# A decoder layer in fp32 on one core: both tiles of an MLP step in one two-bank accumulator, operands and closing norms in larger batches

## The chip, the cores and the metric

The kernel runs on one core of a Trainium2 chip. The metric is the time of one execution on the device in microseconds (us). Before the change three runs took 2319.26, 2319.26 and 2327.7 us, so the median is 2319.26 us.

## What is computed

One step of a hybrid decoder layer on 2048 prompt tokens and 8 single-token samples, all in fp32, width 1024. The first half of the layer mixes tokens (four mLSTM heads of 128 and a causal pooling mixer between an input and an output projection). The second half is the MLP with a hidden width of 4096, which takes most of the time and all of the change:

```python
mix = jnp.einsum('blm,md->bld', mix, w_out)
x = x + ga1 * _rmsnorm(mix, g_post1)

hn2 = _rmsnorm(x, g_pre2) * (1.0 + sc2) + sh2
f = jnp.square(jax.nn.relu(jnp.einsum('bld,df->blf', hn2, w_up)))
f = jnp.einsum('blf,fd->bld', f, w_down)
x = x + ga2 * _rmsnorm(f, g_post2)
```

## The kernel before, in words

**Two phases.** The tokens go in four blocks of 512. Phase one computes the token mixer of all blocks and stores the result x1 in DRAM (`x1_d`). Phase two runs the MLP on block 0 (with the 8 samples joined to it, so its tiles are 260 columns wide where those of the others are 256), then on blocks 1, 2 and 3.

**Seven products.** Each MLP matrix product is done in the block form that needs seven products instead of eight, named P1 to P7. The right operands of the seven are b11, b21, b22 and four sums and differences of quarters of the normed input (`operand_steps`, line 495); the left ones are pieces of the weights, four of which were combined in phase one. `CHAIN` gives each product an accumulator: a takes P1, P6, P7, P4, b takes P2, c takes P5, P3. A product adds to its accumulator and the running sum is read between two products, so the next product on chain a has to wait until the sum before it was read.

**Three matmuls for one.** Every fp32 factor is split into a high and a low half (`split`, line 116: ACT copies the high half, DVE subtracts to get the low one), and every matmul is done as high x high, high x low, low x high. So each weight piece `raw` of 128x1024 gets one ACT copy (`whi`) and one DVE subtraction (`wlo`), with three buffers each.

**The MLP's order.** `mlp_steps` (line 223) writes the order of a block by hand: four chunks of 14 up steps (two groups g0, g1 of seven products) and 14 down steps. A step is 24 matmuls of 256 or 260 columns, or, in the down steps of blocks 1 to 3, 12 of 512. An up step works on two tiles of the hidden width, the pairs, one after the other: `up_step` (line 1351) gives each pair a PSUM bank of its own (`mm` and `ml`, three each), and `up_use` (line 1371) does the vector work of each pair by itself on tiles of 128x256: copies u1, u2, u3 out of chain a, relu squared into `quads`, the sums of the down operands into `sums`, and the halves into `f`. Down products P5, P6, P7 and P3 need the halves of `sums`, which are made only after the up products P4 and P3 of the group. `down_t_step` and `down_step` (lines 1427, 1449) add each result to the tiles `acc`.

**Steps in between.** Generators in the list `steps` are advanced by `tick()` between matmuls. The operands of the next block come that way in four rounds of one pair of k-tiles, begun in the last chunk (line 1531). Block 0's first four operands are made in the last block of phase one (line 1269); for the other three `operand_steps` runs a second time after phase one (lines 1331 to 1333), which loads and norms x1 and transposes its 32 tiles again. The scheduler may move instructions of an engine where the data allow it.

**Closing.** For blocks 1 to 3 `last_adds` (line 1509) squares each finished half tile on ACT, multiplies it on POOL, and `finish_norm` (line 560) takes a reciprocal square root for each 128-token tile by some ten DVE instructions on 128x1 and adds the residual. Block 0's result is transposed, so `finish_t` (line 1476) transposes it back, in one stretch after the block.

Of the kernel before, what the change touches and what calls it, by code (L numbers as in the profile page):

```python
# [17 lines left out]
P = 128  # L18
# [43 lines left out]
def layer_kernel(  # L62
# [30 lines left out]
    ps = ctx.enter_context(tc.tile_pool(name="ps", bufs=3, space=PSUM))  # L93

    def bank(tag, bufs):
        return ps.tile([P, 512], F32, name=tag, tag=tag, bufs=bufs)

    def mm_bank():
        return bank("mm", 3)

    def tr_bank():
        return bank("tr", 2)

    def ml_bank():
        return bank("ml", 3)
# [247 lines left out]
    selb = const.tile([NR, P], F32, name="selb")  # L353
    pool.tensor_copy(out=selb, in_=sel[:, 0:1].broadcast_to([NR, P]))

    warm = const.tile([P, 1], F32, name="warm")
    act.activation(out=warm, in_=one_t, func=AF.Tanh)
    scT = const.tile([P, KT, QP], F32, name="scT")
# [5 lines left out]
    bgate = const.tile([P, 2 * H], F32, name="bgate")  # L364
    gate_w = [const.tile([P, KT, 2 * H], F32R, name=f"gate_w{i}") for i in range(2)]
# [11 lines left out]
    def mod_load(u):  # L377
        raw = fetched.pop(0)
        rt = small.tile([NR, UC], F32, name="rt", bufs=2)
# [78 lines left out]
    def prenorm_steps(part, tiles, sample, xh, xl):  # L458
# [14 lines left out]
        for half in range(2):  # L473
# [4 lines left out]
            for k2 in range(KT // 2):  # L478
# [5 lines left out]
                for kk in range(2):  # L484
                    k = 2 * k2 + kk
                    yt = rows.tile([P, TS // 2], F32, name="yt", bufs=2)[:, :2 * P]
# [8 lines left out]
    def operand_steps(b, ops, products, room):  # L495
# [4 lines left out]
        if sample:  # L500
            xt = scale_rows(load_rows(x1_d[S:], NS), NS)
        xts = [scale_rows(load_rows(src, P), P) for src in x1_tiles(b)]
        for j in products:
            n = X_ORDER.index(j)
            t = (acts.tile([P, H, BUF + TS], F32R, name="uext", bufs=1) if n == PRODUCTS - 1 else
                 acts.tile([P, 4, TS], F32R, name=("hi4", "lo4")[n % 2])).rearrange("p a b -> p (a b)")
            ops[j] = t[:, :8 * SH].rearrange("p (c k t) -> p c k t", c=2, k=4)
        yield
        if sample:
            tp = tr_bank()  # L510
            for k in range(KT):
                pe.transpose(tp[:, k * NS:(k + 1) * NS], xt[:NS, k * P:(k + 1) * P], ident[:NS, :NS])
# [4 lines left out]
        for kt in range(4):  # L517
            top, low, ta, tb = room()
            for k, y in ((kt, top), (kt + 4, low)):
                tp = tr_bank()  # L520
                for i, xt in enumerate(xts):
                    pe.transpose(tp[:, i * P:(i + 1) * P], xt[:, k * P:(k + 1) * P], ident)
                act.activation(out=y[:, :, :HT], in_=tp.rearrange("p (h t) -> p h t", h=2), func=AF.Identity,
                               scale=sc_c[:, 1, k, 0:1], bias=sh_c[:, 1, k, 0:1])
                if sample:
                    pool.tensor_copy(out=y[:, :, HT:], in_=ys[:, k].rearrange("p (h n) -> p h n", h=2))
            yield
            b11, b12, b21, b22 = (y[:, h, :w] for y in (top, low) for h in range(2))
            t1, t2, t3, t4 = (t[:, h, :w] for t in (ta, tb) for h in range(2))
# [3 lines left out]
            if P7 in products:  # L533
                dve.tensor_tensor(out=t3, in0=b22, in1=b12, op=ALU.subtract)
            if P4 in products:
                dve.tensor_tensor(out=t4, in0=b21, in1=t2, op=ALU.subtract)
            for n, j in enumerate(products):
                split(ops[j][:, 0, kt, :w], ops[j][:, 1, kt, :w], src[j])
                if n % 3 == 2:
                    yield  # L540
            yield

# [211 lines left out]
    with tc.tile_pool(name="p1c", bufs=1) as p1c, tc.tile_pool(name="p1", bufs=1) as p1:  # L754
# [99 lines left out]
        def phase_one_room():  # L854
            y = [p1.tile([P, BUF + T], F32, name=n) for n in ("ps_a", "ps_b")]
            y += [p1.tile([P, TS], F32, name="pd", bufs=2) for _ in range(2)]
            return [t[:, :2 * SH].rearrange("p (h t) -> p h t", h=2) for t in y]
# [41 lines left out]
        def sample_heads(q, k, hvs):  # L899
# [53 lines left out]
            num = p1.tile([P, H, HD + 1], F32, name="num", bufs=2)[:NS]  # L953
# [11 lines left out]
            def ready(b):  # L965
# [3 lines left out]
                km = p1.tile([P, H, HD + 1], F32, name="w", bufs=2)[:NS, :, :HD]  # L969
# [33 lines left out]
        for b in range(NB):  # L1003
# [71 lines left out]
            def chunk_weights(c):  # L1075
# [11 lines left out]
                w = p1.tile([P, H, HD + 1], F32, name="w", bufs=2)[:, :, :P]  # L1087
# [26 lines left out]
            def chunk_heads(c, w, ae):  # L1114
                t0, t1 = c * P, (c + 1) * P
                num = p1.tile([P, H, HD + 1], F32, name="num", bufs=2)
# [150 lines left out]
            else:  # L1267
                xops = {}
# [307 lines left out]
```

## Time and profile before

| What | Value |
|---|---|
| median of three runs | 2319.26 us |
| the profiled execution, its own time | 2322.08 us |
| its span in the profile | 2320.4 us |
| mean granted clock of TensorE | 0.972 of full speed |
| phase one's last matmul; PE goes on with block 0 | 890.2 us; 931.6 us |
| block 1, block 2, block 3 begin | 1289, about 1645, about 1985 us |
| last matmul | 2305.6 us |

The profiled execution is 2.8 us longer than the median. [...] Almost all instructions are issued by one helper, so nearly every row names line 54 and the tiles tell which step it is: `raw`, `whi`, `wlo` are weights, `f` the halves of the hidden tiles, `u`, `quads`, `sums` the vector work between, `hi`, `lo`, `uext` the operands, `acc` the sums of the output, `xt` rows of x1, `tr` transposes.

### The profile page before, as it was taken

To read this page: it belongs to the slowest core of one execution; us is meant where nothing else is said; L and a number is where in the kernel's file an instruction comes from. 1 tells how busy PE (TensorE), PEld (TensorE's weight loads), DVE (VectorE), ACT (ScalarE), POOL (GpSimd) and SP (SyncE) were. 2 spreads that over 40 slices of the span, in tenths; PEclk is the share of its full clock that TensorE was granted. 3 is DMA by queue.
4 is the path that set the end of the run, shared out by engine and by line. 5 is a ranking of instruction groups with operands and counts; after the bars stand their busy time and mean duration, and the time that the engine had idled before them with its cause. 6 is when DMAs were issued, how large, how long until landed. Compare 5 with 4: busy or idle time off the path is not lost. (4 is left out here: it accounts for less than half of the span.)

```text
span 2320.4 us, 37926 instructions
## 1 busy us (share of the span) xinstructions
PE 2194.2 (95%) x14106; PEld 1923.7 (83%) x14106; DVE 1757.3 (76%) x3750; ACT 1166.9 (50%) x2047; POOL 114.9 (5%) x169
## 2 busy tenths in 40 slices
PE   7999999999999996899998899998999998999997
PEld 6997788787887775899998888987888987888995
DVE  4356867866784787867778988779978779968878
ACT  4342534533442355654546555546655547555554
POOL 2000000000000000000000300000100000100002
PEclk9997999999999997999999999999999999999998
DMA  8741487489479855465454655655755555655563
GB/s 278 223 144 54 136 294 258 157 274 309 150 223 298 269 167 192 138 193 159 153 188 148 226 185 168 195 184 172 235 192 181 183 184 171 215 190 180 176 224 123
DMA packets 270524, 451.78 MB, mean 195 GB/s; under 512 B 17377, under 2 KB 171146, under 8 KB 270330
## 3 DMA queue, kind: packets, MB, share of 16 engines
q1 hardware_dynamic: 270339, 449.36, 59.8%
q8 instruction: 111, 1.82, 0.3%
q14 instruction: 74, 0.61, 0.1%
HBM read 394.31 MB, written 55.21 MB: 194 GB/s over the span
## 5 line engine op out<-in xcount | busy, mean ns | idle before, releaser
L54 DVE TENSOR_TENSOR wlo<-raw,whi 128x1024 fp32r<-128x1024 f32 (+1 forms) x562 | 691.3, 1236 | 266.2 <-ACT whi L54 255.0
L54 ACT CAST whi<-raw 128x1024 fp32r<-128x1024 f32 (+1 forms) x562 | 585.4, 1047 | 599.0 <-PE ml L54 399.3
L54 PE MATMUL mm<-hi,whi 128*128 128x256 f32 (+2 forms) x1408 | 378.1, 322 | 14.0 <-ACT whi L54 7.8
L54 PE MATMUL mm<-lo,whi 128*128 128x256 f32 (+2 forms) x1408 | 370.8, 316 | 1.5 <-DVE rs_t L54 1.5
L54 PE MATMUL mm<-hi,wlo 128*128 128x260 f32 (+2 forms) x1024 | 336.5, 329 | 6.2 <-DVE wlo L54 6.0
L54 PEld LDWEIGHTS mm<-hi,whi 128*128 128x128 f32 x1408 | 242.4, 191 | 36.6 <-ACT whi L54 10.2
L54 PE MATMUL mm<-whi,f 128*128 128x512 f32 x672 | 246.1, 403 | 14.1 <-ACT whi L54 13.7
L54 PEld LDWEIGHTS mm<-lo,whi 128*128 128x128 f32 x1408 | 242.4, 191 | 19.6 <-ACT whi L54 1.6
L54 PE MATMUL ml<-whi,f 128*128 128x512 f32 x672 | 243.9, 398 | 0.0
L54 PEld LDWEIGHTS mm<-hi,wlo 128*128 128x128 f32 x1024 | 195.4, 191 | 28.3 <-DVE wlo L54 9.9
L54 PEld LDWEIGHTS mm<-whi,f 128*128 128x128 f32 x672 | 126.6, 190 | 56.4 <-ACT whi L54 21.6
L54 PEld LDWEIGHTS ml<-whi,f 128*128 128x128 f32 x672 | 127.2, 189 | 29.7
L54 PE MATMUL ml<-hi,whi 128*128 128x256 f32 (+1 forms) x768 | 142.5, 283 | 3.2 <-ACT u L54 3.2
L54 PE MATMUL mm<-wlo,f 128*128 128x512 f32 x336 | 134.6, 401 | 10.6 <-DVE wlo L54 10.6
L54 PE MATMUL ml<-lo,whi 128*128 128x256 f32 (+1 forms) x768 | 141.9, 282 | 0.0
L54 PE MATMUL ml<-wlo,f 128*128 128x512 f32 x336 | 133.6, 398 | 0.0
L54 PEld LDWEIGHTS ml<-hi,whi 128*128 128x128 f32 x768 | 118.6, 189 | 4.1 <-ACT u L54 4.0
L54 PEld LDWEIGHTS ml<-lo,whi 128*128 128x128 f32 x768 | 118.5, 189 | 0.0
L54 PE MATMUL mm<-lo,wlo 128*128 128x256 f32 (+1 forms) x384 | 109.5, 285 | 1.4 <-DVE wlo L54 1.3
L54 PE MATMUL mm<-f,whi 128*128 128x260 f32 x448 | 96.4, 304 | 13.9 <-ACT f L54 10.9
L54 PE MATMUL ml<-lo,wlo 128*128 128x256 f32 (+1 forms) x384 | 108.6, 283 | 0.0
L54 PE MATMUL ml<-hi,wlo 128*128 128x256 f32 (+1 forms) x384 | 108.6, 283 | 0.0
(383 smaller groups left out, 4439.0 us busy)
## 6 DMA issues: line engine op xcount, KB each, us to landing
raw<-in_w_up_dram SPq DMA_DIRECT2D x128, 512.0 KB
raw<-up_s SPq DMA_DIRECT2D x128, 512.0 KB
raw<-in_w_down_dram SPq DMA_DIRECT2D x104, 512.0 KB
raw<-dn_s SPq DMA_DIRECT2D x96, 512.0 KB
raw<-in_w_in_dram SPq DMA_DIRECT2D x80, 512.0 KB
raw<-in_w_ada_dram SPq DMA_DIRECT2D x32, 512.0 KB
xt<-x_d SPq DMA_DIRECT2D x32, 512.0 KB
raw<-dn_s SPq DMA_DIRECT2D x64, 256.0 KB
```

The lines of the kernel that those rows point to most:

```text
L54: ins = op(*args, **kwargs)
```

## The change

PSUM is dealt anew in phase two: three tiles of two banks, chain0 to chain2, each holding both pairs, instead of six single banks. `turn()` rotates which of them serves as a, b and c. A step's vector work is done once for both pairs, on 128x2x256, after the second pair's matmuls; the tiles u1 to u3 and `quads` give way to `qa` and `qb`. The order of the steps changes, and the halves are written product by product. The operands of blocks 1 to 3 come in two rounds of two k-tiles, with one square-root chain for four tiles (`scale_block`). Block 0's operands are all made inside phase one: five get their halves there, and those of P4 and P3 are kept as fp32 (`held`) and split at its end. Closing norms take two tiles at once, and `finish_t` becomes a step generator that runs beside block 1's up steps.

```diff
-            out += up(g0, P1, P2, P6, P5, P7) + up(g1, P1) + up(g0, P4, P3) + up(g1, P2, P6, P5, P7)
-            if b == 0:
-                out += down((P1, 0)) + up(g1, P4, P3)
-                out += down(*[(j, 0) for j in (P5, P6, P2, P7, P3, P4)])
-                out += down(*[(j, 1) for j in (P1, P5, P6, P2, P7, P3, P4)])
-            else:
-                out += down((P1, 0), (P1, 1)) + up(g1, P4, P3)
-                out += down((P5, 0), (P2, 0), (P6, 0), (P5, 1), (P6, 1), (P2, 1), (P7, 0), (P7, 1),
-                            (P3, 0), (P3, 1), (P4, 0), (P4, 1))
+            parts = [[0], [1]] if b == 0 else [[0, 1]]
+            out += up(g0, P1, P2, P6, P5, P7, P3) + up(g1, P1) + up(g0, P4) + up(g1, P2, P6, P5, P7, P3)
+            for n, part in enumerate(parts):
+                out += down(*[(P1, i) for i in part]) + (up(g1, P4) if n == 0 else [])
+                out += down(*[(j, i) for j in (P5, P6, P2, P7, P3, P4) for i in part])
...
+        now = X_ORDER if held is None else X_ORDER[:5]
...
-        for kt in range(4):
-            top, low, ta, tb = room()
+        for i in range(4 // nk):
+            kts = slice(nk * i, nk * (i + 1))
+            top, low, ta, tb = room(i)
...
+            if held is not None:
+                dve.tensor_tensor(out=b21, in0=b21, in1=t2, op=ALU.subtract)
+                held.append({P4: b21, P3: b22})
...
-                xops = {}
-                steps.append(operand_steps(0, xops, X_ORDER[:4], phase_one_room))
+                xops, held = {}, []
+                steps.append(operand_steps(0, None, xops, phase_one_room, 1, held))
...
         drain()
-        steps.append(operand_steps(0, xops, X_ORDER[4:], phase_one_room))
-        drain()
+        for j in X_ORDER[5:]:
+            xops[j] = operand_tile(j)
+            for kt, y in enumerate(held):
+                split(xops[j][:, 0, kt:kt + 1], xops[j][:, 1, kt:kt + 1], y[j])
...
+        def turn(a, b, c):
+            order.update(zip("abc", [order[x] for x in (a, b, c)]))
+
+        def chain_of(st, j):
+            key = CHAIN[j]
+            if j in OPENS and key not in st:
+                if key == "a":
+                    st["order"] = dict(order)
+                n = f"chain{st['order'][key]}"
+                st[key] = ps2.tile([P, 2, 512], F32, name=n, tag=n)
+            return st[key]
...
             elif j == P2:
...
+                dve.tensor_tensor(out=a11, in0=st["b"][:, :, :w], in1=a11, op=ALU.add)
+                squared_relu(a11)
+                st["f"] = F_of[g % 2] = p2.tile([P, 2, PRODUCTS, 2, SH], F32R, name="f", bufs=2)
+                halves(SLOT[P1], a11)
...
+            elif j == P3:
+                dve.tensor_tensor(out=a21, in0=st["c"][:, :, :w], in1=a21, op=ALU.add)
+                squared_relu(a21)
+                st["t"] = t = p2.tile([P, 4, 2, SH], F32, name="sums")
+                s1, s2, s3 = (t[:, i, :, :w] for i in range(3))
+                dve.tensor_tensor(out=s1, in0=a21, in1=a22, op=ALU.add)
+                halves(SLOT[P5], s1)
+                dve.tensor_tensor(out=s2, in0=s1, in1=a11, op=ALU.subtract)
+                dve.tensor_tensor(out=s3, in0=a11, in1=a21, op=ALU.subtract)
+                halves(SLOT[P6], t[:, 1:3, :, :w], 2)
             elif j == P4:
...
+                act.activation(out=a12, in_=a, func=AF.Relu)
+                act.activation(out=a12, in_=a12, func=AF.Square)
+                halves(SLOT[P2], a12)
+                s2, s4 = (st["t"][:, i, :, :w] for i in (1, 3))
+                dve.tensor_tensor(out=s4, in0=a12, in1=s2, op=ALU.subtract)
+                halves(SLOT[P3], s4)
...
+                eng = dve if last_block and (th, dh) == (1, 0) else pool
+                eng.tensor_tensor(out=dst, in0=dst, in1=ga2_b[dh][:, None, :].broadcast_to([P, 2, 512]), op=ALU.mult)
...
+                ssq = small.tile([P, 2], F32, name="ssq2")
+                dve.tensor_reduce(out=ssq, in_=sqs[th], op=ALU.add, axis=AX.X)
+                r = rsqrt_mean(ssq, D, P, 2)
...
             if b == 0:
-                finish_t(acc)
+                steps.append(finish_t(acc))
```

**ACT at the end of the up steps of block 0's first chunk.** Before, the last up product leaves `sums`, whose four slots for P5, P6, P7 and P3 are cast to halves in one instruction of 1040 columns for each pair, and the second pair's stands behind two copies of the first down result:

```order
L54 CAST whi<-raw 128x1024 x2
L54 ACTIVATE quads<-ml 128x260
L54 CAST f<-sums 128x1040
L54 CAST f<-quads 128x260
L54 ACTIVATE quads<-quads 128x260
L54 CAST f<-quads 128x520
L54 COPY acc_9871<-mm 128x260
L54 COPY acc_9872<-ml 128x260
L54 CAST whi<-raw 128x1024
L54 CAST f<-sums 128x1040
```

Now:

```order
L54 CAST f<-qb 128x520
L54 CAST whi<-raw 128x1024
L54 COPY acc_10111<-chain_10122 128x2x260
L54 CAST f<-sums 128x520
L54 CAST whi<-raw 128x1024
L54 CAST f<-sums 128x1040
L54 ACTIVATE qa<-chain_9872 128x520
L54 ACTIVATE qa<-qa 128x520
L54 COPY acc_10113<-chain_10193 128x2x260
L54 CAST f<-qa 128x520
```

The half for down product P5 (the first `f<-sums`, 520 columns) is cast by itself, for both pairs, and ahead of the relu of up product P4 (`qa<-chain_9872`); those for P6 and P7 (1040 columns) come next.

**PE between the phases.** `hi_9120`, `lo_9121`, `lo_9123` are the operands of P1, P2 and P5, `hi_9122` that of P6. Before:

```order
L54 MATMUL tr<-ident,C 4x128
L54 MATMUL mm<-hi_9120,whi 128x260 x2
...
L54 MATMUL mm<-lo_9121,whi 128x260 x2
...
L54 MATMUL mm<-lo_9123,whi 128x260 x2
...
L54 MATMUL ml<-lo_9123,wlo 128x260
L54 MATMUL tr<-ident,xt 128x8 x8
L54 MATMUL tr<-ident,xt 128x128 x32
L54 MATMUL mm<-hi_9122,whi 128x260 x2
```

Now, with `hi_9050` and `lo_9051` for P1 and P2, `hi_9052` and `lo_9053` for P6 and P5:

```order
L54 MATMUL tr<-ident,xt 128x128 x4
L54 MATMUL mm<-whi,hi_9029 128x512
...
L54 MATMUL tr<-ident,xt 128x128 x12
L54 MATMUL chain_9665<-hi_9050,whi 128x260 x2
...
L54 MATMUL chain_9698<-lo_9051,whi 128x260 x2
...
L54 MATMUL chain_9766<-lo_9053,whi 128x260 x2
L54 MATMUL chain_9665<-hi_9052,whi 128x260 x2
```

The 32 transposes behind the three products are gone. The last 12 of block 0's only transposes stand ahead of P1, and the other 20 lie between matmuls of the output projection (`mm<-whi,hi_9029`).

**DVE at the turn from block 1 to block 2.** Before, these are the rows around the third of the four rounds of operands; from the `f<-sums` ahead of the first round to the row `wlo` below stand 36 rows with no `wlo` in them:

```order
L54 TENSOR_TENSOR acc0_14343<-mm_17490,acc0_14343 128x512
L54 TENSOR_TENSOR lo4_17459<-sums_17612,lo4_17459 128x256
L54 TENSOR_TENSOR hi4_17460<-sums_17612,hi4_17460 128x256
L54 TENSOR_TENSOR lo4_17461<-sums_17612,lo4_17461 128x256
L54 TENSOR_TENSOR acc2_14345<-ml_17507,acc2_14345 128x512
L54 TENSOR_TENSOR wlo_17673<-raw_17594,whi_17672 128x1024
L54 TENSOR_TENSOR uext_17462<-quads_17611,uext_17462 128x256
L54 TENSOR_TENSOR wlo_17707<-raw_17630,whi_17706 128x1024
```

Now, the second of two rounds:

```order
L54 TENSOR_TENSOR wlo_16786<-raw_16715,whi_16785 128x1024
L54 TENSOR_TENSOR lo4_16591<-sums_16701,lo4_16591 128x2x256
L54 TENSOR_TENSOR sums_16701<-qb_16703,sums_16701 128x2x256
L54 TENSOR_TENSOR sums_16701<-qb_16703,qa_16702 128x2x256
L54 TENSOR_TENSOR sums_16701<-qb_16703,sums_16701 128x2x256
L54 TENSOR_TENSOR lo4_16589<-qb_16703,lo4_16589 128x2x256
L54 TENSOR_TENSOR hi4_16590<-sums_16701,hi4_16590 128x2x256
L54 TENSOR_TENSOR acc0_14209<-chain0_16717,acc0_14209 128x2x512
L54 TENSOR_TENSOR uext_16592<-sums_16701,uext_16592 128x2x256
L54 TENSOR_TENSOR hi4_16593<-sums_16701,hi4_16593 128x2x256
L54 TENSOR_TENSOR lo4_16594<-qb_16703,lo4_16594 128x2x256
L54 TENSOR_TENSOR wlo_16810<-raw_16746,whi_16809 128x1024
```

The instructions are twice as wide, and each of the two rounds has ten of them (nine of 512 columns, one `acc` of 1024) between two `wlo`; between the rounds stand two `wlo`.

## Rows read from the trace of the kernel before

**Rows 1.** The page, part 1: busy time, share of the span, instructions.

```profile
PE 2194.2 (95%) x14106; PEld 1923.7 (83%) x14106; DVE 1757.3 (76%) x3750; ACT 1166.9 (50%) x2047; POOL 114.9 (5%) x169
```

**Rows 2.** Busy time by stretch; columns: stretch, length, busy by engine, clock, DMA share, GB/s.

```profile
0.00:890.00 890.00, 858.33 (x5193) 707.86 (x5194) 591.55 (x1667) 371.46 (x816) 51.97 (x119) 0.98 0.66 214
890.00:931.00 41.00, 19.34 (x115) 15.38 (x113) 33.53 (x120) 22.33 (x41) 1.52 (x8) 0.65 0.63 222
1597.00:1660.00 63.00, 51.26 (x274) 43.33 (x273) 61.16 (x139) 41.52 (x80) 13.47 (x8) 0.92 0.63 211
1660.00:1938.00 278.00, 275.55 (x1777) 247.12 (x1777) 223.53 (x363) 157.35 (x230) 0.00 (x0) 1.00 0.58 187
```

**Rows 3.** Timeline of PE between the phases: start, us, what, [idle before <-releaser].

```profile
931.58 0.80 PE L54 MATMUL mm<-hi,whi 128*128 128x260 f32 x2 [5.95 <-ACT u L54]
```

**Rows 4.** Groups of instructions, 899 to 931 us: count | busy, mean ns | idle before.

```profile
L54 PE MATMUL tr<-ident,xt 128*128 128x128 f32 x32 | 9.0, 438 | 10.4 <-DVE xt L54 7.4 <-ACT ps_a L54 3.0
```

**Rows 5.** Waits of PE, 960 to 1289 us: total, times, longest.

```profile
PE mm L54 <- ACT f L54: 10.9, 4, 3.0
```

**Rows 6.** Timeline to the stall at 1057 us in block 0: DVE, ACT, PE.

```profile
1056.71 1.22 DVE L54 TENSOR_TENSOR wlo<-raw,whi 128x1024 fp32r<-128x1024 f32 x1
...
1058.36 0.39 ACT L54 ACTIVATE quads<-ml 128x260 f32<-128x260 f32 x1 [2.22 <-DVE sums L54]
1058.65 1.05 ACT L54 CAST f<-sums 128x1040 fp32r<-128x1040 f32 x1
...
1052.84 0.40 PE L54 MATMUL mm<-uext,whi 128*128 128x260 f32 x2
...
1053.21 0.40 PE L54 MATMUL mm<-uext,whi 128*128 128x260 f32 x2
...
1059.75 0.58 PE L54 MATMUL mm<-f,whi 128*128 128x260 f32 x1 [2.92 <-ACT f L54]
```

**Rows 7.** Stretches of 8 us before and behind such a stall, columns as in rows 2.

```profile
961.00:969.00 8.00, 8.00 (x66) 7.71 (x64) 6.22 (x12) 3.85 (x8) 0.00 (x0) 1.00 0.50 155
1058.00:1066.00 8.00, 6.21 (x26) 5.74 (x27) 6.92 (x14) 3.73 (x7) 0.00 (x0) 0.57 0.20 68
```

**Rows 8.** Groups of DVE and ACT, 1348 to 2300 us.

```profile
L54 DVE TENSOR_TENSOR wlo<-raw,whi 128x1024 fp32r<-128x1024 f32 x320 | 395.1, 1243 | 126.8 <-ACT whi L54 126.3
...
L54 ACT CAST whi<-raw 128x1024 fp32r<-128x1024 f32 x319 | 332.9, 1051 | 331.9 <-PE ml L54 269.4 <-issue 47.7 <-DVE wlo L54 13.8
...
L54 ACT COPY u<-mm 128x256 f32<-128x256 f32 x66 | 24.5, 371 | 16.4 <-PE mm L54 16.2
```

**Rows 9.** Timeline at the turn from block 1 to block 2: DVE, then PE.

```profile
1601.01 2.36 DVE L54 TENSOR_TENSOR wlo<-raw,whi 128x1024 fp32r<-128x1024 f32 x2
...
1607.08 0.42 DVE L54 TENSOR_TENSOR uext<-quads,uext 128x256 fp32r<-128x256 f32 x1
1607.41 0.76 DVE L54 TENSOR_TENSOR hi<-sums,hi 128x256 fp32r<-128x256 f32 x2
...
1613.30 0.69 DVE L54 TENSOR_TENSOR acc<-mm,acc 128x512 f32<-128x512 f32 x1
1613.90 0.69 DVE L54 TENSOR_TENSOR acc<-ml,acc 128x512 f32<-128x512 f32 x1
...
1619.18 1.69 DVE L54 TENSOR_TENSOR wlo<-raw,whi 128x1024 fp32r<-128x1024 f32 x1
...
1613.31 0.50 PE L54 MATMUL mm<-whi,f 128*128 128x512 f32 x1 [2.39 <-ACT whi L54]
...
1620.93 0.79 PE L54 MATMUL mm<-wlo,f 128*128 128x512 f32 x1 [5.28 <-DVE wlo L54]
```

**Rows 10.** Waits of PE, 1660 to 1938 us, then 1289 to 1348 us.

```profile
PE mm L54 <- ACT whi L54: 2.2, 4, 0.7
...
PE tr L54 <- DVE quads L54: 4.9, 4, 1.6
```

**Rows 11.** Timeline of the end: the last matmul.

```profile
2305.58 0.39 PE L54 MATMUL ml<-whi,f 128*128 128x512 f32 x1
```

More of the change, by code (lines that the diff above doesn't have):

```diff
@@ L500, in operand_steps @@
         if sample:
[L501 to L507, printed above, removed]
+            xt_s = scale_rows(load_rows(x1_d[S:], NS), NS)
+        now = X_ORDER if held is None else X_ORDER[:5]
+        for j in now:
+            ops[j] = operand_tile(j)
         yield
@@ L1277, in layer_kernel @@
             for n, w in (("sig", TS), ("uext", BUF + TS)):
+                if n == "uext" and b == NB - 1:
+                    rt = [p1.tile([P, H, HD], F32, name="hv", bufs=4).rearrange("p a b -> p (a b)") for _ in range(4)]
+                    res += [rt[:2], rt[2:]]
+                    continue
                 rt = (acts if n == "uext" else p1).tile([P, H, w], F32, name=n, bufs=1).rearrange("p a b -> p (a b)")
@@ L1451, in down_step @@
+            seen.add(at)
+        def down_step(c, j, part, st, acc, seen, last):
             unit = next_piece(512)
+            if j == P1 and part == 0:
+                turn(*"bac")
+                st.clear()
+            out = chain_of(st, j)
             for pair in range(2):
-                st = state.setdefault(("d", pair), {})
-                key = CHAIN[j]
-                if j in OPENS and part == 0:
-                    st[key] = bank(("mm", "ml")[pair], 3)
-                out = st[key]
@@ L1458, in down_step @@
                 for k in range(2):
-                    f = F_of[part, k]
+                    f = F_of[part]
                     wh, wl = unit[k]
-                    fh, fl = (f[:, i, SLOT[j], pair * P:(pair + 1) * P] for i in range(2))
+                    fh, fl = (f[:, i, SLOT[j], k, pair * P:(pair + 1) * P] for i in range(2))
                     for i, (l, r) in enumerate([(fh, wh), (fh, wl), (fl, wh)]):
-                        pe.matmul(out, lhsT=l, rhs=r, start=j in OPENS and part == k == i == 0,
+                        pe.matmul(out[:, pair], lhsT=l, rhs=r, start=j in OPENS and part == k == i == 0,
@@ L1464, in down_step @@
                                   stop=j in CLOSES and part == k == 1 and i == 2, skip_group_check=True)
                 tick()
-                if part == 0:
-                    continue
-                th, dh = ADDS[j]
-                i = 2 * th + pair
-                dst = acc[2 * i + dh][:, :512]
-                add_to(dst, out, c == 0 and (i, dh) not in seen)
-                seen.add((i, dh))
-                if last is not None and j in {(0, 0): (P2,), (0, 1): (P3,), (1, 1): (P7,), (1, 0): (P4,)}[th, dh]:
-                    last(i, dh, dst)
+            if part == 0:
+                return
@@ L1476, in finish_t @@
+            th, dh = ADDS[j]
+            dst = acc[2 * th + dh][:, :, :512]
+            add_to(dst, out, c == 0 and (th, dh) not in seen)
+            seen.add((th, dh))
+            if last is not None and j == {(0, 0): P2, (0, 1): P3, (1, 1): P7, (1, 0): P4}[th, dh]:
+                last(th, dh, dst)
         def finish_t(acc):
-            compact = p2.tile([P, KT, NS], F32, name="sums")
-            for dt in range(KT):
-                pool.tensor_copy(out=compact[:, dt].rearrange("p (h n) -> p h n", h=2),
-                                 in_=acc[dt].rearrange("p (h t) -> p h t", h=2)[:, :, HT:SH])
+            compact = small.tile([P, KT, NS], F32, name="ys", bufs=1)
@@ L1534, in layer_kernel @@
+                    continue
+                if not acc:
+                    drain()
+                    acc = [p2.tile([P, 2, 2 * SH], F32, name=f"acc{j}") for j in range(4)]
+                if b == 0:
+                    down_t_step(c, *what, downs, acc, seen)
                 else:
-                    down_step(b, c, *what, state, acc, seen, last_adds if c == N_CHUNK - 1 else None)
+                    down_step(c, *what, downs, acc, seen, last_adds if c == N_CHUNK - 1 else None)
             drain()
```

297 lines of the change are left out of this document (162 added, 135 removed).

## The prediction

> **What bounds the kernel now.** I read the share of busy time first [rows 1]: PE is busy for 2194 of 2320 us and DVE for 1757, so PE is the bound and DVE the engine that can starve it. A mean says nothing of places, so the next view is the busy time by stretch [rows 2]. In the middle of block 2 (1660 to 1938 us) PE is busy for 275.6 of 278 us at clock 1.00. The lost time lies elsewhere: between the phases (890 to 931 us) PE is busy for 19 of 41 us at clock 0.65, and at the turn from block 1 to 2 for 51 of 63 us, while DVE is busy for 61 of those 63. The waits of PE in block 0 give a third place: four waits for ACT's `f`, 10.9 us in all [rows 5].
>
> The durations are those of one execution of 2322.1 us (span 2320.4), 2.8 us above the median. The sum is made against 2322 and then shifted.
>
> The price of PE's work: in steady flow three matmuls of 260 columns start within 0.37 us (1052.84 to 1053.21) [rows 6], 0.12 us each, so a step of 24 is 2.9 us.
>
> **A. Between the phases.** PE takes up block 0 at 890.2 us, does three steps (3 x 2.88 = 8.6 us), then stands, transposes the 32 tiles again (9.0 us at 438 ns each [rows 4]) and goes on at 931.58, behind ACT and DVE [rows 3]. So 41.4 us give 8.6 us of MLP: 32.8 us are lost. In the change the reload, the second norm and the 32 transposes are gone. What is late next is DVE: between the last operand round's start and the `wlo` for P6 its order has 17 operand instructions of 260 columns, eight of 512 that finish x1 rows, and some ten single-column ones. With start-to-start times at 1607.08 (0.33) and at 1613.30 (0.60) [rows 9], and 0.2 us taken for the single-column ones, this is 5.7 + 4.8 + 2.0 = 12.5 us; ACT's modulated copies before and two `wlo` bring it to about 18 us after the last transpose. PE has two steps to do meanwhile (5.8 us), so 12.2 us are lost in place of 32.8: 20.6 less. The other 20 transposes now stand among matmuls of a phase where PE is busy for 858 of 890 us [rows 2]; at 0.12 us they cost 2.4. I take **-18**. Bounds: if the x1 rows' loads hold DVE back, -5; if the scheduler's wait is hidden behind P1 and P2 more than I count, -25.
>
> **B. The halves in block 0.** In the stall at 1057 us the chain is: last up product P3, then on DVE a `wlo` (1056.71) in front of the last sum, ACT waits 2.22 us for that sum, then casts 1040 columns (1.05 us), and PE starts P5 at 1059.75 after 2.92 us [rows 6]. Behind such a stall the clock falls: from 1058 to 1066 us the granted clock averages 0.57 and 26 matmuls start, where at full clock 66 did in as long [rows 7]. Of these 8 us 1.75 are the wait; 26 matmuls are worth 3.1 us, so 6.25 - 3.1 = 3.1 us go to the low clock. Four times: 10.9 + 12.4 = 23.3 us. In the change P3 comes before P4, so P4 of the group and the first down step (5.8 us) lie between P3's end and P5, and P5's sum is cast alone. In their way stand on DVE an add, a square, a sum and a subtraction of about 0.6 us and a `wlo`, on ACT a cast: about 5.2 us. It just fits, and a miss of some tenths would not drop the clock: waits of 0.7 us leave it at 1.00 in block 2 [rows 2, 10]. I take **-23**; bounds -15 (two places still miss) and -24.
>
> **C. From block 0 to block 1.** `finish_t` ran in one stretch, with 4.9 us of PE's waits on its `quads` [rows 10]; now it is spread over block 1's up steps, where PE has other work. **-5**, bounds 0 and -8. Its transposes and DVE work stay.
>
> **D. The turns 1 to 2 and 2 to 3.** Before, DVE issues no `wlo` from 1603.4 to 1619.18, and PE waits 5.28 us for one [rows 9]. In the change there are two rounds of ten instructions, each 9 x 0.60 + 1.2 = 6.6 us, with two `wlo` (1.14 to 1.24 us [rows 8]) between. Three `wlo` buffers let DVE be three down steps (2.8 us each) ahead: PE reaches the step that needs the `wlo` behind the second round after about 14.1 us, DVE has it after about 19.0. So one stall of 4.9 us stays, with a clock loss of 3.1, where there were 2.39 + 5.28 [rows 9] and smaller ones after. Closing norms for two tiles halve the single-column chains. I take -3 a turn, **-6**; bounds +5 (both rounds stall) and -8.
>
> [...]
>
> **I. Interior chunks of blocks 1 to 3.** PE's waits there are 2.2 us in 278 [rows 10], about ten chunks of 81 us (those away from turns) make 6.5 us, mostly `whi` behind ACT work that now comes half as often. **-5**, bounds 0 and -6.5. Fewer, wider instructions on DVE and ACT otherwise cost and give nothing: DVE's idle time before `wlo` is 126.8 us of waiting for `whi` [rows 8], so PE does not wait for DVE there. If that cover went, every 1% of the 950 us of blocks 1 to 3 would be 10 us.
>
> **E. The end.** 14.8 us follow the start of the last matmul [rows 11]. Now both last tiles share one norm, one wide DVE multiplication replaces two on POOL, but the norm starts only when both are done: **-1**, bounds -3 and +3.
>
> The rest of phase one is unchanged but for tile names: 0, bounds -3 and +3. Sum: -18 - 23 - 5 - 6 - 5 - 1 = -58, so 2264, and against the median **2261 us**. A measurement of this kernel can tell about 0.5%, 11.6 us, from no change.
>
> **Rivals.**
>
> *Slower: the two-bank tiles are read too late.* Before, a pair's bank was free to be read 12 matmuls (1.4 us) before the step's end, and the next product on chain a, one step later, found its own pair's bank 1.4 + 2.9 = 4.3 us after. Now reading starts when both pairs are done and must end within one step, 2.9 us. ACT needs about 0.6 us for the copy (0.37 for 256 columns now), behind at most a `whi` of 1.05 us and a cast of the halves of 1.05: 2.7 us [rows 6, 8]. It fits, with 0.2 us to spare. There are 14 such reuses in each of 16 chunks, 224. From a mean of 0.26 us each (58 / 224) the gain is gone; at 0.4 us the kernel takes 2261 + 90 = 2351 us. For it: thin margin, engines in order. Against it: such piles of ACT work stand at few of the 14 places, and DVE and ACT have idle time. 0.08.
>
> *The stalls at the turns and between the phases stay.* Loads hold A at -5 and both rounds of D stall (+5): 2261 + 13 + 11 = 2285 us. For it: DVE is full at the turn [rows 2]. 0.12.
>
> *The change does not do what it says at P5.* The scheduler may place `wlo` ahead of the sum, or P4's half, now last, may be late for P2; then B is 0 and with A at -5 it gives 2261 + 23 + 13 = 2297 us. For it: 5.2 of 5.8 us is tight. Against it: ACT's order has P5's cast well ahead of P4's relu. 0.06.
>
> *Small waits at every change of bank hold the clock down.* One stretch such as that in [rows 7] per chunk costs 3.1 x 16 = 50 us: 2311 us. Against it: block 2 has such waits at clock 1.00 [rows 2, 10]. 0.03. [...]
>
> **How the numbers follow.** The forecast has 0.71, with an own range of 2243 to 2290 from the bounds that can come together. Rivals: 0.08, 0.12, 0.06, 0.03. The range of 2238 to 2308 holds the forecast almost whole, the second and the third rival, and leaves out the slower one and the clock. Faster by over 0.5% (under 2307.7): 0.71 + 0.12 + 0.06 less a little for cases of the last two terms at their bounds, 0.86. Within 0.5%: 0.05. Slower: 0.09.
>
> **What would show it.** Right: no wait of PE for `f` over 1 us in block 0 and clock near 1.00 where it was 0.57; P6 starts about 12 us after P2's end, with no `tr<-ident,xt` between the phases; one stall on `wlo` at each turn of 4 to 6 us; mean clock above 0.972; DVE instructions from 3750 to some 3100. Wrong: waits of PE for ACT's `qa` or `qb` or DVE's reads of `chain` all through the interior, which is the slower rival; a hole of over 20 us between the phases; `f` waits still there.

## The result, and the profile after

The changed kernel takes 2243.26 us (median of 4 runs, 2239.35 to 2246.64) beside 2319.26 us before; the ratio is 0.9667 with a 95% interval of 0.9636 to 0.9699. The forecast was 2261 us in a range of 2238 to 2308 us: the direction and the range held, the gain was 76 us instead of 58.

The two traces (spans 2320.4 and 2242.4 us) are compared at a landmark that both have, the first matmul of a chunk's long down run, which starts behind the chunk's last up step and reads the hidden tiles `f`:

| Stretch between landmarks | Before, us | After, us | Gain, us | Term of the forecast |
|---|---|---|---|---|
| start to block 0's first down run | 968.0 | 942.6 | 25.4 | A, 18 |
| three chunk lengths of block 0 | 264.6 | 243.8 | 20.8 | B, 23 for four places |
| block 0's last chunk, on to block 1 | 114.8 | 103.4 | 11.4 | fourth place of B, and C, 5 |
| nine chunk lengths inside blocks 1 to 3 | 725.0 | 713.0 | 12.0 | I, 5 |
| turns 1 to 2 and 2 to 3 | 196.6 | 187.6 | 9.0 | D, 6 |
| from block 3's last down run to the end | 51.4 | 52.0 | -0.6 | E, 1 |

These are single profiles. In seven profiles whose kernels have the same code up to the first landmark (the changed kernel and the six of its variants that touch only later work), that landmark lies between 941.9 and 946.5 us. Before the change six matmuls of P1 still stood behind the landmark; they are worth 0.7 us in block 0 and 1.4 us in the other blocks. With the same work on both sides of it the first and the third row would gain 0.7 us more, and the last would lose 1.4 us more.

First the busy time of the engines over the span, part 1 of the page of the changed kernel [rows 1]:

```profile
PE 2158.3 (96%) x14066; PEld 1909.8 (85%) x14066; DVE 1698.0 (76%) x3047; ACT 1137.6 (51%) x1807; POOL 113.4 (5%) x144
```

DVE has 703 instructions fewer, as foreseen, but its busy time fell by only 59 us and its share not at all. Busy time by stretch of the changed kernel, columns as in [rows 2]:

```profile
0.00:887.00 887.00, 856.65 (x5190) 706.59 (x5190) 590.48 (x1648) 370.58 (x814) 50.37 (x118) 0.97 0.66 213
887.00:903.00 16.00, 7.83 (x56) 6.86 (x56) 15.78 (x46) 10.10 (x23) 0.56 (x1) 0.89 0.88 328
1451.50:1530.20 78.70, 78.70 (x507) 71.29 (x506) 62.25 (x68) 42.28 (x50) 0.00 (x0) 1.00 0.59 188
1530.00:1624.00 94.00, 86.20 (x542) 76.56 (x542) 88.15 (x128) 64.88 (x98) 13.37 (x4) 0.98 0.67 224
```

The third row is a whole chunk inside block 1: PE is busy for all of its 78.70 us at a granted clock of 1.00. The second row is the hole between the phases, now 16 us long with 7.8 us of work in it. The fourth is the turn from block 1 to 2, where DVE is still busy for 88 of 94 us. The waits of PE in block 0 from 940 to 1290 us (total, times, longest), which answer to [rows 5]:

```profile
PE tr L54 <- DVE xt L54: 3.9, 4, 1.4
PE chain L54 <- DVE wlo L54: 1.8, 3, 1.3
PE chain L54 <- DVE acc L54: 1.8, 1, 1.8
PE chain L54 <- DVE f L54: 0.8, 1, 0.8
PE chain L54 <- ACT whi L54: 0.5, 1, 0.5
```

The row of 10.9 us on ACT's `f` is gone. The hole between the phases in the timeline of the changed kernel, ACT and then PE [rows 3]:

```profile
902.25 0.59 ACT L54 COPY qa<-chain 128x520 f32<-128x520 f32 x1 [4.08 <-DVE lo L54]
...
895.06 0.50 PE L54 MATMUL chain<-lo,whi 128*128 128x260 f32 x2
902.90 0.59 PE L54 MATMUL chain<-hi,whi 128*128 128x260 f32 x1 [7.34 <-ACT qa L54]
```

PE finishes P2, does two matmuls of P5 and stands for 7.34 us. It waits for ACT's copy of P1's sum out of chain a, which P6 adds to, and that copy waits for DVE's last `lo`, the low half of one of the operands split last.

### The profile page after: what moved, and what is told of

Read it like the earlier page. It is cut to its first block, busy times and chain, and to the rows that moved or that the text cites. A ratio compares the mean times of both kernels' runs of the same rounds, so it can differ in the third digit from the quotient of the medians.

```text
span 2242.4 us, 36775 instructions
## 1 busy us (share of the span) xinstructions
PE 2158.3 (96%) x14066; PEld 1909.8 (85%) x14066; DVE 1698.0 (76%) x3047; ACT 1137.6 (51%) x1807; POOL 113.4 (5%) x144
## 5 line engine op out<-in xcount | busy, mean ns | idle before, releaser
L54 DVE TENSOR_TENSOR wlo<-raw,whi 128x1024 fp32r<-128x1024 f32 (+1 forms) x562 | 689.2, 1230 | 243.2 <-ACT whi L54 236.7
L54 PE MATMUL chain<-whi,f 128*128 128x512 f32 x1344 | 432.0, 398 | 0.0
L54 PEld LDWEIGHTS chain<-whi,f 128*128 128x128 f32 x1344 | 255.5, 190 | 58.5
L54 PE MATMUL chain<-hi,whi 128*128 128x256 f32 (+1 forms) x1536 | 280.5, 284 | 11.7 <-ACT qa L54 10.9
L54 PE MATMUL chain<-lo,whi 128*128 128x256 f32 (+1 forms) x1536 | 278.8, 282 | 0.0
L54 PE MATMUL chain<-wlo,f 128*128 128x512 f32 x672 | 268.5, 400 | 9.9 <-DVE wlo L54 9.9
L54 PEld LDWEIGHTS chain<-hi,whi 128*128 128x128 f32 x1536 | 239.0, 190 | 14.8 <-ACT qa L54 11.5
L54 PE MATMUL mm<-hi,whi 128*128 128x512 f32 (+1 forms) x640 | 234.2, 366 | 6.0 <-ACT whi L54 5.9
L54 PEld LDWEIGHTS chain<-lo,whi 128*128 128x128 f32 x1536 | 236.1, 188 | 0.2
L54 PE MATMUL mm<-hi,wlo 128*128 128x512 f32 (+1 forms) x640 | 227.4, 357 | 2.4 <-DVE wlo L54 2.3
L54 PE MATMUL mm<-lo,whi 128*128 128x512 f32 (+1 forms) x640 | 226.9, 355 | 0.0
```

The costliest lines, as they stand in the source:

```text
L54: ins = op(*args, **kwargs)
```

## The experiments

Three theories for the blocks stood against each other. O: the place of P3 in the step order made the waits for `f`. Q: the tile `quads` had a single buffer, so the second pair's vector work could start only when the first pair's was finished. W: the number and width of the vector instructions. A fourth, A, concerns the hole between the phases; the others concern the turns.

**A second buffer alone, in the kernel before.** Room for it came from closing phase one's small tiles.

```diff
-                st["q"] = p2.tile([P, 4, SH], F32, name="quads")
+                st["q"] = p2.tile([P, 4, SH], F32, name="quads", bufs=2)
```

> The kernel before, with a second buffer for the tile quads (room for it by freeing phase one's small tiles), steps and banks as before. Theory Q (one quads buffer makes the second pair's vector work wait until the first pair's is done, and this is what the waits for f came from): the waits of PE for f in block 0 fall from 10.9 us to under 3, the low clock behind them goes, and interior chunks lose their waits for whi; about 2290 us (2280 to 2300). Theory O (the place of P3 in the step order made them): waits for f stay at 9 to 11 us, 2312 to 2322 us. Theory W (number of vector instructions): as O.

Measured: 2295.79 us, ratio to before 0.9896 (0.9873 to 0.992). Its waits of PE from 940 to 1230 us, where the kernel before has 7.9 us of waits for ACT's `f`, in three places:

```profile
PE mm L54 <- ACT f L54: 1.6, 3, 0.5
PE mm L54 <- DVE acc L54: 1.3, 2, 0.7
PE mm L54 <- DVE f L54: 1.1, 2, 0.5
PE mm L54 <- ACT acc L54: 0.3, 1, 0.3
```

The waits for `f` are nearly gone with the old order and the old banks (they stay at 1.6 us up to 1289 us, where the kernel before has 10.9). What moved is ACT's relu of the second pair's P4 in the chunk of [rows 6]. In the kernel before it waited there until 1058.36 us for the first pair's last sum, and DVE then had three squares of the second pair in a row:

```profile
1058.30 1.11 DVE L54 SCALAR_TENSOR_TENSOR quads<-u 128x260 f32<-128x260 f32 x3
```

With two buffers that relu runs well ahead of the cast of the sums:

```profile
1054.60 0.37 ACT L54 ACTIVATE quads<-ml 128x260 f32<-128x260 f32 x1
...
1059.31 1.06 ACT L54 CAST f<-sums 128x1040 fp32r<-128x1040 f32 x1 [1.82 <-DVE sums L54]
```

Chunks inside block 1 take 78.8 us instead of 80.8, as in the changed kernel. Theory Q holds for the waits in the kernel before. The chunks of block 0 take 83.2 to 83.7 us, though, where the changed kernel needs 80.7 to 82.3.

**The new order alone, in the kernel before.**

```diff
-            out += up(g0, P1, P2, P6, P5, P7) + up(g1, P1) + up(g0, P4, P3) + up(g1, P2, P6, P5, P7)
+            out += up(g0, P1, P2, P6, P5, P7, P3) + up(g1, P1) + up(g0, P4) + up(g1, P2, P6, P5, P7, P3)
...
+                halves(st["f"], 3, 4, t, w, 3)
```

> The kernel before with only the new step order (P3 two steps ahead of P4, halves written product by product), one quads buffer, a bank for each pair. Theory O: waits for f under 3 us, about 2295 us (2285 to 2300). Theory Q: the second pair's work still starts when the first pair's is done, which is now behind P4, so waits for f stay or grow: 2315 to 2345 us. Theory W: within 5 us of before.

Measured: 2353.43 us, ratio 1.0148 (1.0124 to 1.0172), slower, and above what theory Q gave. All its waits of PE from 940 to 1230 us:

```profile
PE mm L54 <- DVE wlo L54: 10.2, 7, 2.7
PE mm L54 <- ACT whi L54: 0.5, 1, 0.5
```

No wait for `f` is left, as theory O had it and against theory Q, but PE now waits for the weights. The three chunk lengths of block 0 gain 4.9 us (259.7 instead of 264.6), and the nine inside blocks 1 to 3 lose 30.7 (755.7 instead of 725.0). Timeline of DVE in this run, block 1:

```profile
1397.46 1.23 DVE L54 TENSOR_TENSOR wlo<-raw,whi 128x1024 fp32r<-128x1024 f32 x1 [0.18 <-ACT whi L54]
1398.60 0.42 DVE L54 TENSOR_TENSOR sums<-quads,sums 128x256 f32<-128x256 f32 x1
1398.94 0.69 DVE L54 TENSOR_TENSOR f<-quads,f 128x512 fp32r<-128x512 f32 x1
1399.66 1.10 DVE L54 SCALAR_TENSOR_TENSOR quads<-u 128x256 f32<-128x256 f32 x3
...
1405.57 1.22 DVE L54 TENSOR_TENSOR wlo<-raw,whi 128x1024 fp32r<-128x1024 f32 x1
```

When the first pair's last `sums` and `f` are done, the three squares of the second pair follow in a row (`quads<-u` x3), and with all that hangs on them 7.0 us pass between two `wlo` (1398.60 to 1405.57). A down or up step takes PE 2.8 to 2.9 us (12 matmuls that start 0.23 us apart, or 24 at 0.12).

**The old order, in the changed kernel.**

```diff
-            out += up(g0, P1, P2, P6, P5, P7, P3) + up(g1, P1) + up(g0, P4) + up(g1, P2, P6, P5, P7, P3)
+            out += up(g0, P1, P2, P6, P5, P7) + up(g1, P1) + up(g0, P4, P3) + up(g1, P2, P6, P5, P7)
```

> The changed kernel with the old step order (P4 ahead of P3, all halves of the sums behind P3). Theory O: waits for f come back, 2 to 3 us at each of four places with the low clock behind, and waits for whi in every interior chunk: 2265 to 2275 us. Theory Q: both pairs' work is ready together without a wait for a buffer, waits for f under 1.5 us, 2243 to 2252 us. Theory W: within 5 us of the changed kernel.

Measured: 2308.42 us (10 runs), ratio to before 0.9953 (0.994 to 0.9966). All three theories missed: 65 us of the changed kernel's 76 are gone. (The profiled execution took 2317.49 us, the longest of the ten.) Its waits of PE from 940 to 1230 us are not for `f`:

```profile
PE chain L54 <- DVE wlo L54: 5.6, 6, 1.5
PE tr L54 <- ACT qa L54: 1.5, 1, 1.5
PE chain L54 <- DVE acc L54: 1.3, 2, 0.6
PE chain L54 <- ACT whi L54: 0.6, 2, 0.3
```

And DVE in block 1 of this run:

```profile
1469.10 1.22 DVE L54 TENSOR_TENSOR wlo<-raw,whi 128x1024 fp32r<-128x1024 f32 x1
1470.23 0.69 DVE L54 SCALAR_TENSOR_TENSOR qb<-qb 128x512 f32<-128x512 f32 x1
...
1476.90 2.36 DVE L54 TENSOR_TENSOR wlo<-raw,whi 128x1024 fp32r<-128x1024 f32 x2
```

With P4 and P3 next to each other, all the vector work that hangs on them falls into one stretch of 6.7 us without a `wlo`. Now the weights are late, where before the hidden tiles were; in the interior chunk from 1411 us PE waits 1.0 us for `wlo` and 1.0 for `whi`.

**One instruction for each pair, in the changed kernel.** Every vector operation of an up step on 128x2x256 becomes two on 128x256; tiles, banks and order stay.

```diff
-            a11, a12 = (st["qa"][:, h, :, :w] for h in range(2))
+            a11, a12 = (st["qa"][:, h, pr, :w] for h in range(2))
...
+            for pr in range(2):
+                use_pair(st, j, w, pr)
```

> The changed kernel with the vector work of the up steps split into one instruction for each pair (twice as many, 256 or 260 columns wide), tiles, banks and order as changed. Theory W (the gain of 2 us in each interior chunk comes from fewer and wider instructions): interior chunks of 80 to 81 us instead of 78.7, 2265 to 2275 us in all. Theories O and Q: DVE has room, chunks stay at 78.7 to 79.0, 2243 to 2250 us.

Measured: 2280.42 us, ratio to before 0.9832 (0.9809 to 0.9854), 37 us slower than the changed kernel and beyond what theory W gave. A chunk inside block 1:

```profile
1425.00:1505.80 80.80, 79.39 (x507) 71.47 (x506) 63.93 (x99) 43.64 (x72) 0.00 (x0) 1.00 0.57 183
```

Thirty-one more DVE instructions cost only 63.93 - 62.25 = 1.68 us of busy time, 0.05 us each, and DVE is idle for 17 of 81 us. So it is not DVE's throughput that costs 2 us a chunk. PE waits for `wlo` three times from 1380 to 1530 us, 1.9 us in all.

**Order, second buffers and product-by-product halves, but separate banks and instructions, in the kernel before.**

```diff
-            t = p2.tile([P, 4, SH], F32, name="sums")
+            t = p2.tile([P, 4, SH], F32, name="sums", bufs=2)
...
+                st["t"] = t = p2.tile([P, 4, SH], F32, name="sums", bufs=2)
```

together with the edits of the first two runs; the copies u2 and u3 out of chain a go straight into `quads`, and u1 has two buffers instead of three.

> The kernel before with second buffers for quads and sums, the new step order and halves written product by product, but still a bank and a set of instructions for each pair, and the old work between the phases, at the turns and at the end. If order and buffers are what the changed kernel gains in the blocks (theory Q+O): as the changed kernel with the old boundary, 2268 to 2280 us, interior chunks of 78.7 us, block 0's of 80.5 to 82. If the joined instructions are needed for the new order (theory W, as the run with an instruction for each pair suggests): interior chunks of 80 us or more, 2290 to 2315 us.

Measured: 2310.53 us (6 runs), ratio to before 0.9951 (0.9932 to 0.9969): 15 us slower than the second buffer of `quads` with the old order, and chunks inside block 1 take 80.5 us. With the changed kernel's instructions split it was 80.8 us. So the new order needs the joined instructions. Inside blocks 1 to 3 order and joined instructions only pay together, and together they give no more than the second buffer does alone: the nine chunk lengths are 713.0 us in the changed kernel and 710.9 with the second buffer in the kernel before. In block 0 the changed kernel's three are the shorter ones, 243.8 us beside 250.5.

What these seven kernels have in common can be looked for in the timelines, taking in a chunk inside block 1 the longest run of DVE's other work between two `wlo`, and of ACT's between two `whi`:

| Kernel | DVE's longest run, us | ACT's longest run, us | Chunk, us |
|---|---|---|---|
| changed | 3.1 | 2.0 | 78.7 |
| before, second `quads` | 4.3 | 1.7 | 78.8 |
| before, order and second buffers | 4.2 | 2.6 | 80.5 |
| before | 4.3 | 2.9 | 80.8 |
| changed, instructions for each pair | 4.4 | 2.5 | 80.8 |
| changed, old order | 6.6 | 2.0 | 81.8 |
| before, new order | 6.9 | 2.5 | 83.7 |

On the whole the chunk is longer where DVE's run is longer, but at 4.2 to 4.4 us one kernel loses nothing and three lose 2 us. ACT's run tells these apart, 1.7 us beside 2.5 to 2.9. PE's waits in that chunk of the kernel before are for ACT's `whi` (1.0 us, two times), those of the other two for DVE's `wlo` (0.9 us, once, with order and second buffers; 1.9 us, three times, from 1380 to 1530 us with instructions for each pair). This is a pattern over seven kernels. No run changed one of the two lengths alone, so it is not shown that they decide.

**The old work between the phases, in the changed kernel.**

```diff
-                steps.append(operand_steps(0, None, xops, phase_one_room, 1, held))
+                steps.append(operand_steps(0, None, xops, phase_one_room, 1, X_ORDER[:4]))
...
+        steps.append(operand_steps(0, None, xops, phase_one_room, 1, X_ORDER[4:]))
+        drain()
```

> The changed kernel with block 0's operands made as before: four inside phase one, three after it with x1 loaded, normed and transposed again. Theory A (the hole between the phases was the second pass): PE starts the first down run about 25 us later, the rest unmoved, 2268 us (2262 to 2274). Rival (the hole only got shorter because the vector work behind it is joined): within 8 us of the changed kernel.

Measured: 2272.84 us, ratio to before 0.9796 (0.9771 to 0.9822), 29.6 us slower than the changed kernel. Its waits of PE from 890 to 935 us:

```profile
PE tr L54 <- DVE xt L54: 12.7, 2, 8.0
PE chain L54 <- DVE wlo L54: 4.0, 1, 4.0
```

The first down run starts at 974.4 us instead of 942.6, and the rest is unmoved: its three chunk lengths in block 0 are 80.7, 80.7 and 80.8 us. Theory A holds, with more than its 25 us.

**The three batches at the turns, each undone by itself.** First the operands of blocks 1 to 3 in four rounds:

```diff
-                        steps.append(operand_steps(b + 1, scaled, coming, phase_two_room, 2))
+                        steps.append(operand_steps(b + 1, scaled, coming, phase_two_room, 1))
```

> The changed kernel with the operands of blocks 1 to 3 made in four rounds of one k-tile, 256 columns wide, as before, instead of two rounds of two. Theory D (wider instructions relieve DVE at the turns): each of three turns 2 to 6 us longer, 2249 to 2260 us. Rival (four smaller clumps are easier for the weights' three buffers): turns shorter by 1 to 4 us, 2232 to 2241 us.

Measured: 2244.54 us, ratio to before 0.967 (0.9641 to 0.9698). Then block 0's closing in one stretch:

```diff
                 steps.append(finish_t(acc))
+                drain()
```

> The changed kernel with block 0's closing transposes and norms done in one stretch behind the block, not spread over block 1's up steps. Theory C: waits of PE for the transposes' reads come back, 2248 to 2254 us. Rival (DVE has the same work in the same place, so only the order of the waits changes): 2241 to 2247 us.

Measured: 2241.91 us, ratio 0.966 (0.9637 to 0.9683). Then the closing norms tile by tile:

```diff
-                r = rsqrt_mean(ssq, D, P, 2)
+                    r = rsqrt_mean(ssq, D, P, 1)
```

> The changed kernel with the closing norms of blocks 1 to 3 done for each tile by itself as before: POOL multiplies 128x512 at a time, one reciprocal-square-root chain for each of four tiles. Theory N (the batched norms gave the turns their few us): each turn 2 to 4 us longer and the end 1 to 3 us longer, 2248 to 2256 us. Theory T (at the turns DVE is short of time as a whole, and ten small instructions more weigh about 1.5 us a turn): 2243 to 2248 us.

Measured: 2240.89 us, ratio 0.9656 (0.9629 to 0.9683). None of the three can be told from the changed kernel's 0.9667 (0.9636 to 0.9699): the batched operands, the spread closing of block 0 and the batched norms give nothing together with the rest. Only the second result lies in a range that was expected, that of its rival; the first falls between its two and the third below both.

At the end, though, the batched norms cost 4 us. From the start of the last matmul to the end the nine profiles of kernels with the batched norms take 18.6 to 18.8 us; the last run takes 14.7, as the kernel before did (14.8). The changed kernel's last matmul, and what DVE does behind it:

```profile
2223.65 0.40 PE L54 MATMUL chain<-whi,f 128*128 128x512 f32 x1
2227.46 2.74 DVE L54 SCALAR_TENSOR_TENSOR hi<-acc,rs_r,hi 128x512 f32<-128x512 f32 x4
2230.12 1.22 DVE L54 TENSOR_TENSOR acc<-chain,acc 128x1024 f32<-128x1024 f32 x1
```

The same in the last run:

```profile
2223.82 0.40 PE L54 MATMUL chain<-whi,f 128*128 128x512 f32 x1
2224.86 1.41 DVE L54 SCALAR_TENSOR_TENSOR hi<-acc,rs_r,hi 128x512 f32<-128x512 f32 x2
...
2226.51 1.22 DVE L54 TENSOR_TENSOR acc<-chain,acc 128x1024 f32<-128x1024 f32 x1
```

The last sum of the output (`acc<-chain`) stands on DVE behind the norm of the two tiles before it: it starts 6.5 us after the last matmul does, and 2.7 us where the norms come tile by tile. In the median time these 4 us don't show, since the stretch up to block 0's first down run differs by as much from profile to profile.

**Spreading the work of the turn, in the changed kernel.** First the operand work alone, one product for each tick:

```diff
-                if n % 4 == 3:
+                if held is None or n % 4 == 3:
                     yield
```

> The changed kernel with the operand work of the next block released one product at a time over twice as many ticks, so that DVE gets about two of its instructions between two weight pieces instead of ten. If the stall of 4 us at each turn is the clump of ten (theory S): the stall and the low clock behind it go, 6 to 7 us less at each of two or three turns, 2223 to 2233 us. If DVE is short of time over the whole turn (theory T, it is busy nearly all of it): the wait moves to later steps and the time stays within 4 us of the changed kernel.

Measured: 2243.88 us, ratio 0.9672 (0.9644 to 0.97). Busy time in the two halves of the turn from block 1 to 2, in this run:

```profile
1524.70:1565.00 40.30, 37.05 (x173) 29.64 (x172) 38.44 (x43) 31.51 (x50) 6.40 (x3) 0.97 0.59 198
1565.00:1621.70 56.70, 51.01 (x366) 48.98 (x366) 51.44 (x86) 33.05 (x47) 5.21 (x2) 0.93 0.67 231
```

and in the changed kernel:

```profile
1530.20:1573.00 42.80, 39.02 (x179) 31.37 (x178) 38.41 (x45) 31.83 (x50) 9.92 (x3) 0.96 0.61 202
1573.00:1623.40 50.40, 46.38 (x362) 44.48 (x361) 48.95 (x82) 32.45 (x47) 3.46 (x2) 1.00 0.72 245
```

The longest wait of the turn moved. In the changed kernel it stands in the down run:

```profile
1557.78 0.50 PE L54 MATMUL chain<-wlo,f 128*128 128x512 f32 x1 [3.78 <-DVE wlo L54]
```

Now it stands in the next block's up steps:

```profile
1579.89 0.46 PE L54 MATMUL chain<-lo,wlo 128*128 128x256 f32 x1 [3.84 <-DVE wlo L54]
```

The down run is no shorter for it, 42.7 us in both, as three smaller waits came into it: PE is idle for 3.25 us of the 40.30 in its row. The whole turn takes 97.0 us instead of 93.2, and the clock averages 0.93 in its second half. DVE is busy for 89.9 of 97.0 us. The turn from block 0 to 1 takes 99.8 us instead of 103.4, so the total stays. Then the closing work put off into the next block, and both together:

```diff
                 steps.append(finish_t(acc))
+            steps.extend(closings)
```

> The changed kernel with the reciprocal square roots and the residual additions of blocks 1 and 2 put off from the turn into the first up steps of the next block. Theory T (DVE short of time at the turns): some 7 us of DVE work leave the worst place, 3 to 5 us less at each of two turns, 2233 to 2238 us. Rival (they already run in idle time of DVE): 2241 to 2246 us.

> The changed kernel with both: the closing work put off as in the run before, and the operand work of the next block released one product at a time. Theory T: the stall that moved behind the turn when only the operand work was spread now finds DVE with less to do, and the down run keeps its full clock: 2225 to 2235 us. Rival: the sum of DVE work still falls into the same 60 us, 2240 to 2246 us.

Measured: 2245.35 us (0.9672, 0.965 to 0.9694) and 2241.66 us (0.9655, 0.9633 to 0.9677): no gain that can be told. Theory T holds as far as spreading goes, DVE is short of time over the whole turn; its forecast that 7 us moved out of the turn would help was wrong: with the closing work put off, the turns take 95.3 and 94.1 us beside 93.2 and 94.4, and where the 7 us went was not followed up. No run beat the changed kernel clearly.

## Why the prediction was right, and where it was not

**A** was mis-sized: 18 forecast, 25.4 by the landmarks and 29.6 by the run that undoes it, at and past the bound of 25. The order of events was right: PE does P1 and P2 and then waits behind DVE's 32 instructions. What failed is the term of 18 us after the last transpose and 12.2 us lost: PE goes on 15.9 us after the last transposes begin (886.99 to 902.90) and loses 7.34. It waits for ACT's copy of P1's sum, not for P6's `wlo` as I had put it. That copy writes a tile of phase two and waited for DVE's last read of phase one's held tiles; that the two share memory would fit, but it was not tried. The 2.4 us for the 20 transposes inside phase one don't show: PE starts block 0 at 887.40 us, where it did at 890.2.

**B** came near its size, 20.8 us in three chunks for 17 or 18 of the 23, but only part of its working stands. The waits for `f` went and the low clock behind them: the granted clock over these three chunks is 1.00 where it was 0.97, and one wait of 0.8 us is left. The new order by itself does end the waits for `f`, as forecast. What failed is "It just fits" as the whole account of DVE, with nothing for weights that come late: with the order alone, PE waits 10.2 us for `wlo` in block 0 where nothing was forecast, 4.9 of the 20.8 us are gained there, and the kernel as a whole loses 34. The change gains because the joined instructions come with the order; without either it loses 37 to 65 us. Nor was the order the only cure: in the kernel before, `quads` with one buffer made PE wait, which I had read past. A second buffer alone took the waits from 10.9 to 1.6 us. (The terms listed for the 5.2 us, four of 0.6, a `wlo` and a cast of 1.05 at most, make 4.7.)

**I** was mis-sized: 5 forecast, 12.0 measured. I counted idle time of PE as the profile lists it, 2.2 us in 278 [rows 10]. In one chunk before the change (1428 to 1509 us), the wait for `whi` that is listed as 0.67 us stretches the distance between two matmul starts from 0.23 to 1.07 us, by 0.84:

```profile
1447.71 0.40 PE L54 MATMUL ml<-whi,f 128*128 128x512 f32 x1
1448.78 0.50 PE L54 MATMUL mm<-whi,f 128*128 128x512 f32 x1 [0.67 <-ACT whi L54]
```

The matmuls of the chunk's down steps start 0.239 us apart on average where the changed kernel has 0.232. The right measure was the chunk length, 80.8 us, against steps at full rate, 78.7. And the source of these waits was not only ACT work that "comes half as often": the second buffer, which leaves ACT's instructions as they are, gives 14.1 us in the same nine chunks.

**D** came out near its size, 9.0 for 6, but not for its reasons. Neither wider operand instructions nor batched norms carry it. With the old order the two turns take 99.0 and 99.2 us instead of 93.2 and 94.4, with an instruction for each pair 97.6 and 95.8, so it belongs to the up steps' vector work. Of the stall of 4.9 us that I left at each turn, the longest wait for `wlo` is 3.8 us. (The working of the 4.9 doesn't add up either: two rounds of 6.6 us and three `wlo` make 16.9 us, not 19.0, which would leave 2.8.) **C**, the spread closing of block 0, gave nothing: done in one stretch, the same part of the trace takes 104.2 us beside 103.4. What this part gained beyond a fourth place of B, some 4 or 5 of 11.4 us, goes with the up steps' vector work too: it takes 118.1 us with the old order and 110.1 with an instruction for each pair. **E** had the wrong sign: 1 us of gain forecast for the time behind the last matmul, 4.0 us of loss measured (18.8 us instead of 14.8), past the bound of 3, because DVE does the norm of two tiles ahead of the last sum. In the table a down run that is 3.4 us shorter hides it (1.4 of them are the six matmuls that stood behind the landmark).

**The rivals.** Two-bank tiles read too late: not seen in the interior, where with the new order and joined instructions no wait for a read of a chain stands and PE is busy for 78.70 of 78.70 us. The rival's mechanism does show where ACT is held up, in the 7.34 us of the hole and in a wait of 1.9 and of 1.7 us for `qa` behind the two turns. The stalls at the turns stayed, at 3.8 and 3.7 us, the one between the phases did not. At P5 the change does what it says. The clock held down by small waits: not seen either, it is 1.00 in the chunks inside block 1 of the seven kernels of the table, those with waits of 0.9 to 1.0 us among them. What one DVE instruction more costs by itself was a small matter: 0.05 us with an instruction for each pair (1.68 us for 31), next to the 0.06 us that the start-to-start times of [rows 9] give (2 x 0.33 against 0.60) and not the 0.15 of the durations (2 x 0.42 against 0.69). The instructions' number mattered more than that, 37 us in all, which the prediction did not have; the waits for `wlo` that came with it point to where the instructions stand.

## What to carry to other kernels

Before blaming the order of steps for a late operand, look for a tile with one buffer that two independent pieces of work take in turn: nothing in the step order shows it, and here a second buffer was worth a third of the gain by itself. Where engines feed the bottleneck piece by piece, look at the longest stretches between two pieces on each of them, and not only at their totals: here, with an instruction for each pair, DVE was idle for 17 of a chunk's 81 us and its pieces still came late, and two changes (order, joined instructions) paid only together. That the stretches decide is a pattern of these runs, not shown. Where an engine is busy for nearly all of a region (DVE at the turn, for 87.4 of 93.2 us), regrouping or spreading its work there moved the wait and left the time. And batching work at the very end can cost: the last piece then stands behind the batch (here 18.8 us pass from the last matmul's start to the end, instead of 14.8).

## What the runs showed of the hardware

In the case above, in the kernel before, a matmul that waited briefly lost 0.17 us more than the idle time listed (0.84 for 0.67). Joining DVE instructions in pairs, most of them of 256 columns into one of 512, saved 0.05 us of DVE's busy time for each in a chunk inside block 1 (62.25 us with 68 instructions beside 63.93 with 99).
